# A planner's clock for DMA transposes, and one gate item moved in an encoder trunk

## The chip, the cores and the metric

The kernel runs on one core of a Trainium2 chip. The metric is the device time of one execution in microseconds (us); lower is better. Times are given as the median of several runs. Beside them one execution was taken by the hardware profiler, and all rows below come from that one.

The engines of a core are named PE (TensorE, matmuls), PEld (its weight loads), DVE (VectorE), ACT (ScalarE), POOL (GpSimd) and SP (SyncE). In this kernel SP issues every DMA, in the order of its instruction stream; SPq marks such an issue.

## The reference, cut to what matters

A bidirectional encoder of two layers is applied with the same weights to two groups of requests, each of 512 rows of 1024 columns, all in float32:

```python
def encoder_layer(x, c, ...):
    shift, scale, gate = split(silu(c) @ w_ada + b_ada, 3)
    h = rmsnorm(x, g_norm) * (1 + scale) + shift
    qa, ka, va, ga, qb, kb, vb, gb = split(h @ w_in)      # 512 x4, 256 x2, 512 x2 columns
    # mixer A: 8 heads of 64, rotary; three dilated windows, merged by their softmax denominators
    ya = merged(dilated_attention(rope(qa)/8, rope(ka), va, w, d)
                for w, d in ((128,1), (512,4), (2048,16))) * silu(ga)
    # mixer B: 4 heads, key 64, value 128; decaying retention forward + backward, group RMS norm
    r = retention(rope(qb), rope(kb)/8, vb, decay_fwd) + reversed retention(decay_bwd)
    yr = r * rsqrt(mean(r*r)) * silu(gb)
    return x + gate * (concat(ya, yr) @ w_out)

def trunk(x, c, ...):                                     # for x_prompt and x_sample
    for l in range(2): x = encoder_layer(x, c, ...)
    return rmsnorm(x, g_final)
```

## The kernel before, in words

**Numbers and matmuls.** A float32 factor is split into a high and a low part that TensorE multiplies quickly; a product takes three matmuls (high x high, high x low, low x high). The split of a weight tile is one ACT copy (`wH`) and one DVE subtraction (`wL`). Activations stand transposed in `hT`, one pair of tiles for each k (eight of them) and batch b (two).

**Items.** The input projection of a layer is cut into 20 items, written out in `ORDER0` (layer 0) and `ORDER1` (layer 1): `p` a pair of attention heads' q and k, `v` the same pair's values, `r` and `w` the q, k and the values of two retention heads, `g` a gate. For each item and batch PE runs "main" matmuls from `hT` and the item's weights: a gate item has 24 for each batch (eight k's, three matmuls each). Items are taken in the order of the list; weights are loaded (`loader`) and split (`prepper`) in the same order. The last three items run batch by batch, all of batch 0 first. Then the out projection follows (`wo`, `yT`), 48 matmuls for each tile of 128 rows.

**Background.** What follows from an item is written as generators that are spawned when its main matmuls are issued: `rope` rotates q and k, stores them in DRAM (`stk_dram`) and loads them again as stacks (`QS`, `KS`, `KL`); `attn` multiplies scores; `soften` takes the exponential, writes the probabilities as two 16-bit tiles `pt` and issues a DMA transpose of each, `pT<-pt`; `attn_pv` multiplies the transposed probabilities with the transposed values (`vn<-vt`, also a DMA transpose) in a group of 24 matmuls; `value`, `rvalue`, `ret`, `r_out` and `gate` are the others. `mod_task` computes modulation vectors from `w_ada` tiles (`wa`) in eight steps for each of two tasks; they start at list positions `EX0` = 4 and `EX1` = 9 of layer 0. `outputs` spawns the loads and splits of `w_out` (`rawo`, `wo`) and the splits of y (`yT`) at list position 15 (`LN - LATE`).

**The planner.** Every engine's stream is fixed when the kernel is built. `Engine` passes each instruction on and tells `Plan.note` its estimated cost; `Plan.free` holds the time at which each engine's queue is free by that clock, `Plan.ready` when a tile is there. Before each step of main work `pump` issues background steps whose conditions hold by that clock. A condition is a time: `plan.at(tiles)` is the time at which the tiles are there and a slack by their maker, 1500 ns for a DMA (`SLACK`). The DMA part of the clock is one number, `Plan.dma`, the end of the last booked transfer: an ordinary issue books its bytes after it (an issue costs 450 ns, or 650 ns where neither side is in DRAM), and its landing is 770 ns later. So the clock sets the order of all queues, PE's above all, and what the chip does with that order is not fed back.

Buffers are heaps: `NHALF` = 48 tiles of 4 KB a partition, of which `W_T` may hold 10 (transposes and their sources), and 8 PSUM banks, 5 for main work and 3 for the background.

Of the kernel before, what the change touches and what calls it, by code (L numbers as in the profile page):

```python
# [27 lines left out]
NHALF = 48  # L28
NTURN = 10
NSURE = 3  # L30
ORDER0 = "g0 p0 g4 g5 v0 r0 w0 p1 v1 r1 w1 p2 v2 p3 v3 g1 g6 g7 g2 g3"
ORDER1 = "p0 v0 g0 r0 w0 p1 v1 g1 r1 w1 p2 v2 p3 v3 g4 g5 g6 g7 g2 g3"
EX0 = 4
EX1 = 9
# [113 lines left out]
class Plan:  # L148
# [37 lines left out]
        t = self.soon(*tiles)  # L186
        return 0.0 if t <= self.free[eng] else t

    def note(self, eng, cost, outs, ins, nbytes=0.0):
        part = eng == "SP" and (outs[0].shape[0] < P or outs[0].tensor.name.startswith("stk"))  # L190
        outs = [k for a in outs for k in self.keys(a)]
        ins = [k for a in ins for k in self.keys(a)]
        start = self.free[eng]
        for k in ins:
            start = max(start, self.seen(eng, self.ready.get(k)))
        for k in outs:
            if not (part and self.last.get(k, (0.0, ""))[1] == "DMA"):
                start = max(start, self.seen(eng, self.last.get(k)))
        if self.dead.intersection(outs + ins):
            raise RuntimeError("use of a spare buffer")  # L200
        end = start + cost
        self.free[eng] = end
        if eng == "SP":
            self.dma = max(end + 650.0, self.dma) + nbytes
            end = self.dma + 770.0
            eng = "DMA"
        for k in outs:
            self.ready[k] = (max(end, self.ready.get(k, (0.0, ""))[0]), eng)
        for k in outs + ins:
            if end >= self.last.get(k, (0.0, ""))[0]:  # L210
                self.last[k] = (end, eng)
# [190 lines left out]
class Engine:  # L402
# [5 lines left out]
    def __getattr__(self, op):  # L408
        fn = getattr(self.eng, op)

        def call(*args, **kw):
            r = fn(*args, **kw)  # L412
            outs = [a for k, a in kw.items() if k in self.OUT and hasattr(a, "tensor")]
            ins = [a for k, a in kw.items() if k not in self.OUT and hasattr(a, "tensor")]
            pos = [a for a in args if hasattr(a, "tensor")]
            if "out" in kw:
                ins += pos
            else:
                outs = pos[:1] + outs
                ins = pos[1:] + ins  # L420
            nbytes = 0.0
            if self.name == "SP":
                nbytes = outs[0].free_size() * outs[0].shape[0] * (2.0 / 290.0 if outs[0].dtype == F16 else 4.0 / 345.0)
            self.plan.note(self.name, self.cost(op, outs, ins), outs, ins, nbytes)
            return r
        return call

    def cost(self, op, outs, ins):
        out = outs[0]
        n = out.free_size()  # L430
        psum = any(a.tensor.name.startswith("banks") for a in ins)
        if self.name == "PE":
            c = 0.4219 * n
            self.strip, last = -1, self.strip
            if op == "transpose":
                return max(108.0, 2 * c)
            if ins[0].dtype == F32:
                if out.shape[0] > 32:
                    return max(4 * c, 60.0)
                self.strip = out.offset // out.ap[0][0] // 32  # L440
                return 27.0 if self.strip > last >= 0 else 4 * c
            return 0.5 * c if out.shape[0] == 64 else c + 12.0
        if self.name == "DVE":
            wide = [a for a in ins if a.free_size() > 1]
            fast = len(wide) <= 1 and not psum and op != "tensor_reduce"
            if op == "tensor_reduce":
                n = wide[0].free_size()
            extra = 0.0
            if n > 64 and not psum and (op == "scalar_tensor_tensor" or fast):
                extra = 65.0 * sum(1 for a in ins if a.free_size() == 1) + (60.0 if fast else 0.0)  # L450
            return 66.0 + n * (0.53 if fast else 1.05) + extra
        if self.name == "ACT":
            extra = sum(1 for a in outs[1:]) + sum(1 for a in ins if a.free_size() == 1)
            return (53.0 if psum else 93.0) + 93.0 * extra + 0.833 * n
        if op == "dma_start_transpose":
            return 1250.0 * n / 1024
        return 450.0 if any("dram" in str(a.tensor.name) for a in ins + outs) else 650.0


# [1 line left out]
def trunk_kernel(  # L461
# [364 lines left out]
    KINDS = {"p": "PQK", "v": "PV", "r": "RQK", "w": "RV", "g": "G"}  # L826
    ITEMS = [[(KINDS[x[0]], int(x[1])) for x in order.split()] for order in (ORDER0, ORDER1)]
    EARLY = 4
# [656 lines left out]
```

## Time and profile before

| | |
|---|---|
| median of 3 runs | 1066.94 us (1066.64 to 1071.24) |
| the profiled execution's own time | 1068.72 us |
| its span | 1066.9 us |
| granted TensorE clock over the span | 0.999 of full speed |
| PE busy | 1043.9 us, 5476 matmuls |
| PEld busy | 829.9 us |
| DVE busy | 766.8 us |
| ACT busy | 465.3 us |
| q1, the queue of all these DMAs | 188.69 MB, 62.4% of 16 DMA engines' time |
| DMA transposes | 64 `pT<-pt`, 8 `vn<-vt` |

Busy is the time in which an engine has at least one instruction under way; matmuls overlap, so the sum of their durations is more. The span is the time from the first to the last instruction of the execution that was profiled; its own time has 1.8 us around the span. Stretches are given in us from the start of the span. Layer 0's input projection ends at about 474 us, its out projection at about 565 us; layer 1's input projection ends at about 971 us.

### The profile page before, as it was taken

Reading aid. Unit: us, or ns where it says so; the run is one execution under the profiler, and the core shown is the slowest. Engines: PE = TensorE matmul, PEld = TensorE weight load, DVE = VectorE, ACT = ScalarE, POOL = GpSimd, SP = SyncE. Lnnn points to the kernel's source line nnn. Section 1 sums busy time; section 2 is a strip of 40 time slices with the busy share of each in tenths; the row PEclk is TensorE's granted clock in tenths of the full one; section 3 lists DMA queues with packets and bytes.
Section 4 is the critical chain, followed back from the end, with each engine's and each line's share of the span. In section 5 each row is a group of like instructions: output and inputs, shape, how many; then the busy total and the mean of one; then the engine's idle time right before and its main releaser. Section 6 shows DMA issues by size and latency. Waiting matters only on the chain.

```text
span 1066.9 us, 14779 instructions
## 1 busy us (share of the span) xinstructions
PE 1043.9 (98%) x5476; PEld 829.9 (78%) x5476; DVE 766.8 (72%) x1578; ACT 465.3 (44%) x807; POOL 0.2 (0%) x4
## 2 busy tenths in 40 slices
PE   8999999999999998999999999999999999999997
PEld 4778687777767876778888878878888787778886
DVE  5587766699668896674457885589857897776555
ACT  6364424326432565571234552427433375753011
POOL 0000000000000000000000000000000000000000
PEclk9999999999999999999999999999999999999999
DMA  8747895259964699933221796047941669962222
GB/s 350 295 139 180 238 302 209 73 194 260 273 228 139 160 244 241 234 110 137 89 90 62 240 208 221 21 139 195 244 154 51 224 119 261 244 166 99 97 101 79
DMA packets 209143, 189.63 MB, mean 178 GB/s; under 512 B 156656, under 2 KB 156944, under 8 KB 209072
## 3 DMA queue, kind: packets, MB, share of 16 engines
q1 hardware_dynamic: 209072, 188.69, 62.4%
q8 instruction: 43, 0.70, 0.3%
q14 instruction: 28, 0.23, 0.1%
HBM read 117.34 MB, written 33.57 MB: 141 GB/s over the span
## 4 chain that ended last, share of the span: by engine, by line
PE 77%; DVE 10%; DMA 6%; ACT 2%; SPq 2%; issue 2%; ACTq 0%; DVEq 0%
PE banks L412 77%; SPq L412 2%; DMA wa<-in_w_ada_dram 2%; DVE sS L412 2%; DMA pT<-pt 2%; DVE sd L412 1%; DVE pt L412 1%; DMA KL<-stk_dram 1%; DVE wL L412 1%; DVE yr L412 1%; ACT pt L412 1%; DVE rc L412 1%; DVE rs L412 1%; DVE rsq L412 1%; ACT wH L412 1%
## 5 line engine op out<-in xcount | busy, mean ns | idle before, releaser
L412 PE MATMUL banks<-hT,wH 128*128 128x512 f32 x1536 | 478.7, 392 | 0.6 <-DVE hT L412 0.2
L412 PEld LDWEIGHTS banks<-hT,wH 128*128 128x128 f32 x1536 | 285.3, 188 | 74.4 <-issue 14.1
L412 PE MATMUL banks<-hT,wL 128*128 128x512 f32 x768 | 299.2, 390 | 1.3 <-DVE wL L412 1.3
L412 PE MATMUL banks<-wo,yT 128*128 128x512 f32 (+1 forms) x792 | 175.8, 383 | 0.0
L412 PEld LDWEIGHTS banks<-hT,wL 128*128 128x128 f32 x768 | 144.2, 188 | 32.0 <-DVE wL L412 1.8
L412 PEld LDWEIGHTS banks<-wo,yT 128*128 128x128 f32 x792 | 145.2, 188 | 28.9
L412 PE MATMUL banks<-wH,hT 128*128 128x256 f32 x512 | 97.5, 284 | 0.0
L412 PEld LDWEIGHTS banks<-wH,hT 128*128 128x128 f32 x512 | 81.8, 191 | 4.8 <-issue 3.8
L412 ACT ACTIVATE sS<-sS,sm 128x512 f32<-128x512 f32 x100 | 71.1, 712 | 32.9 <-DVE sm L412 31.9
L412 DVE SCALAR_TENSOR_TENSOR pt<-sS,sm,pt 128x512 f16<-128x512 f32 x100 | 69.9, 747 | 5.0 <-DMA stk_dram<-rs 2.6
L412 PE MATMUL banks<-wL,hT 128*128 128x256 f32 x256 | 72.4, 283 | 0.0
L412 DVE TENSOR_TENSOR wL<-raw,wH 128x1024 fp32r<-128x1024 f32 x56 | 68.1, 1219 | 5.2 <-ACT wH L412 5.1
L412 ACT ACTIVATE wH<-raw 128x1024 fp32r<-128x1024 f32 x56 | 58.5, 1053 | 24.8 <-DMA raw<-in_w_in_dram 23.3
L412 ACT ACTIVATE pt<-sS,sm 128x512 f16<-128x512 f32 x100 | 65.8, 709 | 8.0 <-DVE sm L412 7.0
L412 DVE CUSTOM_DVE_ANT_0 sS<-banks,tabs 128x512 f32<-128x512 f32 x100 | 64.6, 685 | 5.7 <-PE banks L412 5.5
L412 ACT ACTIVATE sq<-xr 128x1024 bf16<-128x1024 f32 (+2 forms) x18 | 17.3, 963 | 116.4 <-DVE xr L412 92.0
L412 DVE TENSOR_TENSOR res<-banks,gb 128x512 f32<-128x512 f32 (+1 forms) x33 | 22.1, 671 | 55.1 <-PE banks L412 55.1
L412 PE MATMUL banks<-pT,vn 128*64 128x512 f16 x384 | 46.0, 381 | 5.4 <-DMA pT<-pt 5.4
L412 PEld LDWEIGHTS banks<-wL,hT 128*128 128x128 f32 x256 | 49.0, 191 | 1.0
L412 PE MATMUL banks<-sr,rv 128*128 128x512 f32 x164 | 46.0, 394 | 0.0
L412 PEld LDWEIGHTS <-vn 128*64 128x64 f16 x384 | 21.3, 109 | 27.4 <-issue 11.8
L412 PE MATMUL banks<-QS 128*128 128x512 f32 x96 | 38.1, 396 | 0.1
(309 smaller groups left out, 1215.7 us busy)
## 6 DMA issues: line engine op xcount, KB each, us to landing
raw<-in_w_in_dram SPq DMA_DIRECT2D x56, 512.0 KB, 4.7
wa<-in_w_ada_dram SPq DMA_DIRECT2D x48, 512.0 KB, 6.8
QS<-stk_dram SPq DMA_DIRECT2D x48, 256.0 KB, 4.5
KS<-stk_dram SPq DMA_DIRECT2D x48, 256.0 KB, 5.1
KL<-stk_dram SPq DMA_DIRECT2D x45, 256.0 KB, 4.6
stk_dram<-rs SPq DMA_DIRECT2D x36, 256.0 KB, 2.9
rawo<-in_w_out_dram SPq DMA_DIRECT2D x16, 512.0 KB, 4.5
stk_dram<-rc SPq DMA_DIRECT2D x24, 256.0 KB, 5.0
```

Source lines behind the costliest of these rows:

```text
L412: r = fn(*args, **kw)
```

## The change: what it does

- `Plan.note` gets a flag for DMA transposes. For one, the queue of SP is taken as occupied until the later of its own cost and 770 ns after the end of all booked transfers; the transfers are then booked until 1400 ns after that, and the tile is there 2200 ns after it. Before, a transpose was booked as any transfer: its queue was free after its cost, and its bytes (0.5 MB, 1.81 us) were added to the booked transfers.
- The cost of a transpose goes from 1250 to 1175 ns for each 1024 columns; both kinds of tile have 2048.
- In layer 0's list the item `g1` stands between `v1` and `r1`, no more between `v3` and `g6`. `EX0`, `EX1` and `LATE` stay as they are. `ORDER1` is not touched.

```diff
-ORDER0 = "g0 p0 g4 g5 v0 r0 w0 p1 v1 r1 w1 p2 v2 p3 v3 g1 g6 g7 g2 g3"
+ORDER0 = "g0 p0 g4 g5 v0 r0 w0 p1 v1 g1 r1 w1 p2 v2 p3 v3 g6 g7 g2 g3"
...
-    def note(self, eng, cost, outs, ins, nbytes=0.0):
+    def note(self, eng, cost, outs, ins, nbytes=0.0, turned=False):
...
         end = start + cost
         self.free[eng] = end
-        if eng == "SP":
+        if eng == "SP" and turned:
+            self.free[eng] = end = max(end, self.dma + 770.0)
+            self.dma = end + 1400.0
+            end += 2200.0
+            eng = "DMA"
+        elif eng == "SP":
             self.dma = max(end + 650.0, self.dma) + nbytes
             end = self.dma + 770.0
             eng = "DMA"
...
-            self.plan.note(self.name, self.cost(op, outs, ins), outs, ins, nbytes)
+            self.plan.note(self.name, self.cost(op, outs, ins), outs, ins, nbytes, op == "dma_start_transpose")
...
         if op == "dma_start_transpose":
-            return 1250.0 * n / 1024
+            return 1175.0 * n / 1024
```

## Rows read from the trace of the kernel before

**Rows 1.** The page: engines' busy us, share of the span, instructions.
```profile
PE 1043.9 (98%) x5476; PEld 829.9 (78%) x5476; DVE 766.8 (72%) x1578; ACT 465.3 (44%) x807; POOL 0.2 (0%) x4
```

**Rows 2.** Busy us of each engine (and instructions) in the last stretch.
```profile
1060.00:1067.00 7.00, 0.00 (x0) 0.00 (x0) 2.74 (x14) 1.23 (x3) 0.00 (x0) 0.79 0.20 75
```

**Rows 3.** PE's waits: us, times, longest; whole span, last line 270 to 310.
```profile
PE banks L412 <- DMA pT<-pt: 5.4, 5, 2.3
...
PE banks L412 <- DMA KL<-stk_dram: 1.7, 3, 1.1
...
PE banks L412 <- DMA wa<-in_w_ada_dram: 1.9, 2, 1.6
```

**Rows 4.** Timeline of PE: start, us, instruction, count, idle before and releaser.
```profile
299.67 2.21 PE L412 MATMUL banks<-wa,siluT 128*32 128x512 f32 x8 [1.62 <-DMA wa<-in_w_ada_dram]
...
407.15 0.62 PE L412 MATMUL banks<-pT,vn 128*64 128x512 f16 x4 [0.69 <-DMA pT<-pt]
410.07 2.32 PE L412 MATMUL banks<-pT,vn 128*64 128x512 f16 x19 [2.31 <-DMA pT<-pt]
...
414.00 0.51 PE L412 MATMUL banks<-KL,QS 128*128 128x512 f32 x1 [1.07 <-DMA KL<-stk_dram]
...
436.39 2.35 PE L412 MATMUL banks<-pT,vn 128*64 128x512 f16 x20 [1.84 <-DMA pT<-pt]
```

**Rows 5.** Tiles pT, then raw: issue ns min/median/max; us to landing.
```profile
L412 SPq DMA_TRANSPOSE pT<-pt x64: 1597/2661/6569, 84.8 to 940.8; - x64
...
DMA to landing us min/median/max: 4.2/4.6/8.3
...
L412 SPq DMA_DIRECT2D raw<-in_w_in_dram x56: 328/424/1191, 5.5 to 915.8; - x56
...
DMA to landing us min/median/max: 3.4/4.7/10.6
```

**Rows 6.** Timeline of SP's DMA issues, two stretches: start, us occupied, count.
```profile
264.61 0.53 SPq L412 DMA_DIRECT2D stk_dram<-th  x1
...
273.72 1.68 SPq L412 DMA_DIRECT2D wa<-in_w_ada_dram  x2
275.49 13.13 SPq L412 DMA_TRANSPOSE pT<-pt  x4
...
386.85 0.92 SPq L412 DMA_DIRECT2D QS<-stk_dram  x2
...
390.30 0.60 SPq L412 DMA_DIRECT2D raw<-in_w_in_dram  x1
391.00 5.23 SPq L412 DMA_TRANSPOSE pT<-pt  x1
```

**Rows 7.** Timeline of PE: two steps (one k each) of a gate item.
```profile
414.35 0.62 PE L412 MATMUL banks<-hT,wH 128*128 128x512 f32 x2
...
415.03 0.62 PE L412 MATMUL banks<-hT,wH 128*128 128x512 f32 x2
```

**Rows 8.** Busy us in stretches: PE, PEld, DVE, ACT, POOL; clock, DMA share, GB/s.
```profile
227.00:257.00 30.00, 30.00 (x145) 22.37 (x144) 29.59 (x66) 16.69 (x34) 0.00 (x0) 1.00 0.93 220
...
257.00:342.00 85.00, 82.48 (x484) 61.59 (x483) 60.74 (x104) 34.28 (x57) 0.00 (x0) 1.00 0.75 223
342.00:400.00 58.00, 58.00 (x268) 46.78 (x267) 54.63 (x122) 32.92 (x68) 0.00 (x0) 1.00 0.79 208
400.00:474.00 74.00, 68.03 (x331) 52.27 (x330) 50.03 (x90) 42.74 (x73) 0.00 (x0) 1.00 0.86 203
```

**Rows 9.** Last PV group and first out projection of layer 0; splits of wo and y.
```profile
453.87 2.78 PE L412 MATMUL banks<-pT,vn 128*64 128x512 f16 x24
...
474.39 10.82 PE L412 MATMUL banks<-wo,yT 128*128 128x512 f32 x47
...
L412 DVE TENSOR_TENSOR wo<-rawo,wo x8: 1217/1219/1225, 439.6 to 472.3; 128x1024 fp32r<-128x1024 f32 x8
...
L412 DVE TENSOR_TENSOR yT<-yr,yT x9: 679/684/687, 474.0 to 483.2; 128x512 fp32r<-128x512 f32 x9
```

## The prediction

> **What bounds the kernel now.** I read the engine totals first: PE is busy 1043.9 of 1066.9 us [rows 1], so at most 23.0 us of the span are idle time of TensorE, and no edit of an order removes a matmul. The last 7 us, without any PE work [rows 2], are the last norm and the stores. What is idle at the start lies before the change can act on the clock, since the first transpose is issued at 84.8 us [rows 5]. What is left is read from the list of PE's waits: 5.4 us on `pT` (a transposed probability tile), 1.7 us on `KL`, and 1.9 us on `wa` around 270 to 310 us [rows 3], together 9.0 us. That is the whole prize. The timeline of PE shows where most of it lies, all in layer 0: 1.62 us at 299.67, 0.69 and 2.31 us in one group of 24 PV matmuls at 406 to 412, 1.07 us on `KL` just behind it, and 1.84 us in the next PV group at 436.39 [rows 4]. PE runs its stream in the order that the planner wrote. A PV group that stands too early in it therefore stops everything behind it, main matmuls that were ready included.
>
> Then the queue of SyncE. A transpose occupies its issuer for 1.6 to 6.6 us (median 2.66), an ordinary 512 KB load for 0.33 to 1.19 us (median 0.42), while both land at a median of 4.6 and 4.7 us [rows 5]. The long ones stand behind ordinary transfers: four transposes behind two `wa` loads hold the queue for 13.13 us, one behind a `raw` load for 5.23 us [rows 6]. The clock of the kernel before gives each 2.50 us (1250 ns per 1024 columns, 2048 columns), whatever is ahead. So the planner believes that the queue is free, and the tiles landed, earlier than they are.
>
> **The change part by part.**
>
> *The clock.* It removes and adds no instruction; it changes what the planner believes, and so the order of every queue after the first transpose. I work its hold out for two bursts, with the kernel's own constants (256 KB book 0.76 us of transfer, 512 KB 1.52 us, the first starts 0.65 us after its issue ends, a landing is 0.77 us later). Burst at 275.49: between 264.61 and 275.4 twelve 256 KB and three 512 KB transfers are issued, of which the first and the last stand in [rows 6], 12 x 0.76 + 3 x 1.52 = 13.7 us from about 265.7, so the last lands at 280.15 by the clock. The first transpose is held 280.15 - 275.49 = 4.66 us, the other three 2.35 us each: 11.7 us, against 10.0 by the old clock and 13.13 in the trace. The new clock finds 1.7 of the missing 3.1 us. The landing of the last moves less: old 288.7 (a transpose booked 1.81 us of transfer and the 0.77 us), new 287.2 + 2.2 = 289.4, a gain of 0.7 us. Burst at 391.00: six 256 KB loads and one of 512 KB from 386.85 [rows 6] run by the clock to 394.0, so the hold is 3.8 us against 2.5 old and 5.23 measured: 1.3 of 2.7 us found, and the landing moves only from 396.7 to 397.0. So about half of the hold becomes visible for what is queued behind a transpose, and a third or less for the tile itself. A PV group also has 1.5 us of slack in its condition (`SLACK`), which covers the rest in the first burst and not where such errors add up, as from 391 to 412.
>
> What each wait is worth by that:
> - `wa` at 270 to 310, 1.9 us: it is queued behind the 13.13 us burst and needs the queue, not the tile; 1.7 us are now foreseen. I take 1.8 gained, bounds 0 and 1.9.
> - `pT` around 291, the part of the 5.4 us that the named groups of [rows 4] leave (5.4 - 4.84 = 0.56): 0.4 gained, bounds 0 and 0.6.
> - `pT` at 406 to 436, 4.84 us: a quarter, 1.2, because landings move by 0.3 to 0.7 us a burst; bounds 0 and 4.8.
> - `KL`, 1.7 us, queue again: half, 0.9; bounds 0 and 1.7.
>
> The sum is 1.8 + 0.4 + 1.2 + 0.9 = 4.3 us. When a wait goes, a main matmul stands in its place and nothing is late next at once, since 0.68 us of ready main work stand for every three matmuls [rows 7]. A re-dealt order can also put a tile earlier than it lands elsewhere, because an unhindered transpose now lands after 2.35 + 2.2 = 4.55 us instead of 2.50 + 0.65 + 1.81 + 0.77 = 5.73. Measured are 4.2 at the least and 4.6 in the median [rows 5], which the slack covers; I take 0, between a gain of 0 and a loss of the same size as the waits that stay, 4.7 us.
>
> *The gate.* g1 is 48 matmuls of 128x512, sixteen steps of 0.68 us: 10.9 us of PE [rows 7]. They move from behind v3 to between v1 and r1, with one 512 KB weight load on SyncE's queue, the split of that weight on ACT and DVE, and two gate tasks, all of which are done at the old place today and cost the same at the new one; the queue loses the load behind v3, where it is held by transposes, and has it ahead of r1. The list positions move with it: the second modulation task still starts behind v1, and the loads of `w_out` are spawned one item earlier in the list, before v3, which in time is the same place because everything from r1 on stands 10.9 us later. Where it goes, DVE has no room (29.59 of 30.0 us) and has been the limit for the background work, so main matmuls are welcome there. Behind that DVE idles: 60.74 of 85 us, then 54.63 of 58, then 50.03 of 74 [rows 8]. Where it leaves, PE has 10.9 us less main work to cover the attention of pair 3. Its cost there is bounded by 0 (the cover lasts) and 10.9 us (the attention stays as far behind v3 as it was). I take 0: the last PV group starts at 453.87, the out projection at 474.39 [rows 9], so a shift of 10.9 us still ends before it, and DVE has 24.0 idle us in that stretch.
>
> Sum: -4.3 us, nothing for the gate. The profiled execution took 1068.72 us with a span of 1066.9; the median of the runs is 1066.94, so I take the sum off that: **1062.6 us**.
>
> **The rivals.**
>
> *All of the idle goes.* The gate puts 10.9 us of main work where DVE was full, bursts fall behind other loads, and PV groups come after their tiles everywhere: 1066.9 - 9.0 = 1057.9 us; I put it at 1058.5. For it: it is ten waits of 2.3 us at most [rows 3]. Against it: the clock still sees only half of a hold.
>
> *The waits stay.* What is late is not what the clock now sees: 1066.9 us. For it: the landing estimates move by 0.3 and 0.7 us only, and groups of [rows 4] were late by more. Against it: each of these waits stands behind a held queue. The Trainium skill, "Advanced Engine Details and Errata", section on the X-bar transpose, says that transposes are as fast as regular DMAs on this chip; by that the hold would be no property of the transpose and the sum would be 0. The trace agrees on the time to landing, 4.6 against 4.7 us, and not on the time at the issuer, 2.66 against 0.42 us [rows 5].
>
> *Slower: the out projection waits for its inputs.* The eight splits of `w_out` on DVE need the heap space that the attention holds, and the last starts at 472.3; nine splits of y tiles follow from 474.0, while PE begins the out projection at 474.39 [rows 9]: its inputs come just in time already. If the attention of pair 3 keeps its distance to v3, all of them come 10.9 us later, and an earlier PE only waits longer. The end then moves by the shift less what DVE's idle time takes back: with half of it taken back the out projection starts 5.5 us later than before, 1066.9 + 5.5 = 1072.4, with nothing taken back 1077.8. The kernel gets slower than before from the point where the first y tiles are split later than 474 us. Against it: the 24.0 idle us of DVE ahead of that point.
>
> **How the numbers follow.** Chances: forecast 40%, all idle goes 27%, waits stay 15%, slower 18%. Less than 0.5% (5.3 us, 1061.6 to 1072.3) is what a measurement of this kernel can't tell from no change. The forecast's own range is 1060.5 to 1065.5, and a fifth of it lies under 1061.6: faster 27 + 8 = 35%, within 32 + 15 = 47%, slower 18%. The range reaches from 1057.5, where nearly the whole 9.0 us are gone, to 1071, which leaves out most of the slower case and a little of the fastest.
>
> **What would show it.** Right: the list of PE's waits no longer has `wa` in layer 0 and has some 3 us of `pT` left; the out projection of layer 0 starts some 4 us before 474.4; layer 1, whose list is the same, hardly changes. The clock is wrong if transposes behind loads no longer hold the queue, or if `pT` waits stay at 5 us or grow. The gate is wrong if PE idles between the last gate matmul and the first `wo` matmul of layer 0, on `yT` or `wo`. The whole is wrong if new waits of several us appear in layer 1, where I price the re-dealing at 0.

## The result and the profile after

The kernel after takes 1058.81 us (median of 6 runs, 1057.38 to 1061.97), the kernel before, run beside it, 1067.62 us (6 runs, 1066.64 to 1072.65). The ratio is 0.9912, 95% interval [0.9887, 0.9938]: 0.9% faster. The profiled execution took 1060.97 us with a span of 1059.1, so the medians differ by 8.8 us and the spans by 7.8.

The page of the kernel after, its span and engine totals, against [rows 1]:

```profile
span 1059.1 us, 14785 instructions
...
PE 1044.4 (99%) x5476; PEld 829.1 (78%) x5476; DVE 765.5 (72%) x1578; ACT 462.5 (44%) x803; POOL 0.2 (0%) x4
```

PE does the same 5476 matmuls in the same busy time (1044.4 against 1043.9 us). What shrank is its idle time. PE's waits in the kernel after from 75 us on (us in total, times, longest), against [rows 3]:

```profile
PE banks L417 <- DMA KS<-stk_dram: 0.6, 1, 0.6
PE banks L417 <- DMA pT<-pt: 0.4, 1, 0.4
PE banks L417 <- DMA KL<-stk_dram: 0.4, 1, 0.4
PE banks L417 <- DMA wa<-in_w_ada_dram: 0.2, 1, 0.2
```

That is 1.6 us against 9.0: 7.4 of the 7.8 us by which the span is shorter. Ten waits became four, and the longest is 0.6 us. PE's timeline shows where the time came from. First the start of layer 1's main matmuls in the kernel before, then what answers to it and to [rows 4, 9] in the kernel after (start, us, instruction, count, idle time before and its releaser):

```profile
565.07 0.62 PE L412 MATMUL banks<-hT,wH 128*128 128x512 f32 x2
```

```profile
284.69 1.05 PE L417 MATMUL banks<-wa,siluT 128*32 128x512 f32 x4 [0.17 <-DMA wa<-in_w_ada_dram]
...
398.02 2.78 PE L417 MATMUL banks<-pT,vn 128*64 128x512 f16 x24
...
425.55 2.78 PE L417 MATMUL banks<-pT,vn 128*64 128x512 f16 x24
...
463.24 4.24 PE L417 MATMUL banks<-wo,yT 128*128 128x512 f32 x18
467.41 2.78 PE L417 MATMUL banks<-pT,vn 128*64 128x512 f16 x24
470.12 6.19 PE L417 MATMUL banks<-wo,yT 128*128 128x512 f32 x26
...
556.85 0.62 PE L417 MATMUL banks<-hT,wH 128*128 128x512 f32 x2
```

Layer 1 begins at 556.85 instead of 565.07: 8.2 us earlier, so the whole gain is made by the end of layer 0, and layer 1 gives 0.4 back. (About 0.7 us of it stands ahead of 75 us, where no transpose has been issued yet: PE waits 4.7 us there against 5.4, so that part is not the change's.) A PV group of 24 matmuls now runs in one piece of 2.78 us; the groups of [rows 4] were broken by waits. The last PV group of layer 0 stands inside the out projection, behind 18 of its matmuls, and nothing waits there.

The queue of SyncE did not get shorter. The transposes of tile `pT` (issuer's ns min/median/max, against [rows 5]) and two single ones on SP in the kernel after:

```profile
L417 SPq DMA_TRANSPOSE pT<-pt x64: 1565/2617/6341, 84.6 to 934.3; - x64
```

```profile
265.32 4.45 SPq L417 DMA_TRANSPOSE pT<-pt  x1
...
273.36 5.23 SPq L417 DMA_TRANSPOSE pT<-pt  x1
```

A transpose holds its issuer as long as before (median 2617 against 2661 ns), and single ones behind loads still take 4.45 and 5.23 us. The chip does the same; what changed is how far PE's stream stays behind it (numbers under the step that failed).

DVE, on the other hand, still has no room where the gate went. Busy us in stretches of the kernel after (PE, PEld, DVE, ACT, POOL with instructions; granted clock, DMA share, GB/s), against [rows 8]:

```profile
227.00:257.00 30.00, 30.00 (x141) 22.22 (x140) 29.53 (x69) 19.12 (x41) 0.00 (x0) 1.00 0.95 251
257.00:342.00 85.00, 84.78 (x497) 65.07 (x496) 57.69 (x95) 30.09 (x49) 0.00 (x0) 1.00 0.72 212
```

### The profile page after: what moved, and what is told of

Same layout as the page of the kernel before. It is cut to its first block, busy times and chain, and to the rows that moved or that the text cites. A ratio compares the mean times of both kernels' runs of the same rounds, so it can differ in the third digit from the quotient of the medians.

```text
span 1059.1 us, 14785 instructions
## 1 busy us (share of the span) xinstructions
PE 1044.4 (99%) x5476; PEld 829.1 (78%) x5476; DVE 765.5 (72%) x1578; ACT 462.5 (44%) x803; POOL 0.2 (0%) x4
## 4 chain that ended last, share of the span: by engine, by line
PE 83%; DVE 7%; DMA 5%; SPq 2%; ACT 1%; issue 1%; ACTq 0%; DVEq 0%
PE banks L417 83%; SPq L417 2%; DMA KL<-stk_dram 1%; DMA stk_dram<-rc 1%; DVE pt L417 1%; DVE hT L417 1%; DVE sd L417 1%; DMA wa<-in_w_ada_dram 1%; DVE sS L417 1%; DVE rc L417 1%; DVE wL L417 1%; ACT wH L417 1%; DMA raw<-in_w_in_dram 1%; DMA stk_dram<-yr 0%; DMA x<-in_x_prompt_dram 0%
## 5 line engine op out<-in xcount | busy, mean ns | idle before, releaser
L417 PE MATMUL banks<-wo,yT 128*128 128x512 f32 (+1 forms) x744 | 165.7, 383 | 0.0
L417 PEld LDWEIGHTS banks<-wo,yT 128*128 128x128 f32 x744 | 136.2, 188 | 27.4 <-ACT wH L417 0.4
L417 ACT ACTIVATE sS<-sS,sm 128x512 f32<-128x512 f32 x90 | 63.9, 712 | 25.0 <-DVE sm L417 24.6
L417 DVE CUSTOM_DVE_ANT_0 sS<-banks,tabs 128x512 f32<-128x512 f32 x90 | 58.9, 685 | 12.3 <-PE banks L417 6.2
L417 DVE SCALAR_TENSOR_TENSOR pt<-sS,sm,pt 128x512 f16<-128x512 f32 x90 | 63.6, 745 | 0.4 <-ACT pt L417 0.4
L417 ACT ACTIVATE pt<-sS,sm 128x512 f16<-128x512 f32 x90 | 59.6, 709 | 2.8 <-DVE sm L417 1.8
L417 ACT ACTIVATE sq<-xr 128x1024 bf16<-128x1024 f32 (+2 forms) x15 | 14.2, 944 | 94.4 <-DVE xr L417 65.1
L417 PEld LDWEIGHTS banks<-sr,rv 128*128 128x128 f32 x166 | 30.5, 188 | 8.5 <-issue 2.5
```

## The experiments

Theory H (the hold): a transpose keeps SyncE's queue until the transfers ahead have landed; the new clock sees it, so what is queued behind comes in time, and that is the gain. Rival N (no hold): only the tile's landing counts, and any order that places PV groups later does as well. Rival G (the gate): the gate's place is what pays. Rival D (the deal): any small change of the clock deals a new order, and the result is one draw. Waits below are PE's from 75 us on, as for the kernel after; their sum stood at 9.0 us before. Ratios are to the kernel before, with their 95% intervals.

### The hold by itself

**e4_hold_alone** leaves out the whole computation: groups of 0 to 4 loads of 512 KB, then three transposes of the kernel's size, then one load behind them, all on SP's queue, twice over.

```python
for i in range(n):
    nc.sync.dma_start(raw[i], w_in[0, (step + i) % 28])
for a, b in zip(src, dst):
    nc.sync.dma_start_transpose(out=b..., in_=a...)
nc.sync.dma_start(fol, w_in[1, step % 28])
```

> A program that leaves out the whole computation: three transposes of one 128x2048 16-bit tile each, directly behind 0, 1, 2, 3 or 4 loads of 512 KB on the same queue, then one load, each group after the one before has landed. If a transpose holds its issuer until the transfers ahead have landed: the first of three takes about 2 us with nothing ahead and then 1.5 us more for each load ahead, some 4, 5.5, 7 and 8.5 us; the second and third take 1.6 to 2.7 us in every group; the load behind starts only after all three. If the hold is the transpose's own cost and chance: the first takes the same 1.6 to 3 us whatever is ahead.

SP's timeline, the first transpose behind 0, 1, 2, 3 and 4 loads (start, us at the issuer):

```profile
4.12 1.42 SPq L488 DMA_TRANSPOSE pT<-pt  x1
...
16.00 3.39 SPq L488 DMA_TRANSPOSE pT<-pt  x1
...
29.37 4.28 SPq L488 DMA_TRANSPOSE pT<-pt  x1
...
44.53 5.71 SPq L488 DMA_TRANSPOSE pT<-pt  x1
...
62.97 5.91 SPq L488 DMA_TRANSPOSE pT<-pt  x1
...
73.85 0.60 SPq L489 DMA_DIRECT2D behind<-in_w_in_dram  x1
```

The second pass gives 1.80, 3.51, 4.34, 6.49 and 6.91 us. Each issue ends with the landing of the last load ahead: 16.00 + 3.39 = 19.4, and that load, issued at 15.55, landed 4.0 us later, at 19.6; for four loads 62.97 + 5.91 = 68.9 against 61.22 + 7.8 = 69.0. The other two transposes of a group take 1.8 to 3.6 us each (7.13 us for three with nothing ahead); all but one of them end within 0.5 us of the landing of the transpose ahead, as at 21.47 against 21.52. The load behind starts only after all three, at 73.85. So the hold exists, and it is one of the queue, not of the tile: the transposes read nothing that the loads wrote. H stands on this point. The size expected per load ahead, 1.5 us, was 2.0 and 1.7 us for the first load and on average 0.8 and 1.1 for each further one (first and second pass).

### The two parts alone

**e1_clock_only**, the kernel after with the old list:

```diff
-ORDER0 = "... v1 g1 r1 w1 p2 v2 p3 v3 g6 g7 g2 g3"
+ORDER0 = "... v1 r1 w1 p2 v2 p3 v3 g1 g6 g7 g2 g3"
```

> The new clock with the gate item at its old place. If the clock alone brings the gain (what PE waits for is tiles behind a held queue, and an order that knows the hold has no such waits), about 1059 us and under 2 us of PE waits on DMAs after 80 us. If the two parts need each other, most of the DMA waits go but a new wait of 3 to 4 us stands near the start of the second retention (about 257 us, where the main matmuls have run out of the background's results and g1 would have filled in), and the time is 1061 to 1064 us. If the order was only dealt anew and came out lucky, anything, with DMA waits of several us at other places.

Measured: 0.9951 [0.9934, 0.9968], 1061.7 us. PE's waits, its timeline (the place of the waits, then a PV group), and SP's queue ahead of them:

```profile
PE banks L417 <- DMA wa<-in_w_ada_dram: 2.3, 2, 1.6
PE banks L417 <- DVE wL L417: 1.3, 1, 1.3
PE banks L417 <- DMA pT<-pt: 0.2, 1, 0.2
```

```profile
274.59 1.05 PE L417 MATMUL banks<-wa,siluT 128*32 128x512 f32 x4 [1.64 <-DMA wa<-in_w_ada_dram]
...
276.28 1.05 PE L417 MATMUL banks<-wa,siluT 128*32 128x512 f32 x4 [0.64 <-DMA wa<-in_w_ada_dram]
...
418.07 2.78 PE L417 MATMUL banks<-pT,vn 128*64 128x512 f16 x24
```

```profile
264.74 5.52 SPq L417 DMA_TRANSPOSE pT<-pt  x1
...
270.31 1.05 SPq L417 DMA_DIRECT2D wa<-in_w_ada_dram  x2
```

The profiled execution, 1065.12 us, is the slowest of its five. The clock alone removes the `pT` waits (5.4 to 0.2 us) and those on `KL`. What is left, 3.6 of 3.8 us, is one place between 264 and 276 us, at the second retention's values: their split `wL` comes late, and then `wa`, which was issued behind a transpose that held the queue for 5.52 us. This is the second of the expected cases, in place, size and time. The PV group of 406 us [rows 4], the sixth of layer 0, now stands at 418.07.

**e2_gate_only**, the kernel before with the new list:

> The gate item at its new place with the old clock. If the gate alone brings the gain: about 1059 us. If the clock is what counts: DMA waits of PE of 5 us or more stay, 1065 to 1069 us. The slower rival of the prediction (the out projection waits for its inputs, since 10.9 us less main work cover the last pair's attention) would show here: a wait on wo or yT of 5 to 9 us at the start of layer 0's out projection, and 1070 us or more.

Measured: 1.0039 [1.0024, 1.0054], 1071.35 us, slower than before. Waits 9.1 us, of which 5.9 on `pT`. PE's timeline at the end of layer 0's list, SP's just ahead of it, and the stretch behind in busy us:

```profile
473.68 0.40 PE L412 MATMUL banks<-pT,vn 128*64 128x512 f16 x1
...
477.64 1.06 PE L412 MATMUL banks<-pT,vn 128*64 128x512 f16 x4 [3.55 <-DMA pT<-pt]
...
480.16 4.16 PE L412 MATMUL banks<-pT,vn 128*64 128x512 f16 x19 [1.46 <-DMA pT<-pt]
```

```profile
464.27 6.01 SPq L412 DMA_DIRECT2D raw<-in_w_in_dram  x4
...
472.58 5.06 SPq L412 DMA_TRANSPOSE pT<-pt  x2
```

```profile
477.00:484.00 7.00, 4.91 (x23) 2.29 (x22) 2.02 (x3) 2.22 (x5) 0.00 (x0) 0.51 0.40 74
```

The last PV group of pair 3 stands inside the out projection and stops it for 5.0 us: its transposes were issued at 472.58, behind four loads. Then 19 of its matmuls take 4.16 us, against 2.32 in [rows 4], at a granted clock of 0.51. So the gate by itself, with the old clock at 1250, does harm, and G as the whole cause falls.

### Later places alone

**e3_slack_3us**, the kernel before with every DMA's slack at 3.0 us, so that each consumer is placed later and no hold is known:

```diff
-SLACK = {..., "DMA": 1500.0}
+SLACK = {..., "DMA": 3000.0}
```

> The kernel before with 3.0 us of slack on every DMA-made tile in place of 1.5. If what matters is only that a PV group is placed later, the waits on pT go as well as with the new clock and the time comes within 2 us of it, 1058 to 1061 us. If the clock must know the hold, because the loads behind a transpose (wa, KL, KS) and the sum of several holds are late by more than 3 us, waits of 3 us or more stay and the time is 1063 to 1067 us.

Measured: 1.0016 [1.0002, 1.003], 1068.51 us. The waits fall from 9.0 to 5.0 us, and the time does not. PE's timeline, SP's queue ahead of it, and busy us in the stretch (the column behind POOL's is the granted clock):

```profile
297.38 0.62 PE L412 MATMUL banks<-pT,vn 128*64 128x512 f16 x4 [1.98 <-DMA pT<-pt]
...
300.43 4.42 PE L412 MATMUL banks<-pT,vn 128*64 128x512 f16 x19 [2.42 <-DMA pT<-pt]
```

```profile
287.03 10.83 SPq L412 DMA_TRANSPOSE pT<-pt  x3
```

```profile
298.60:305.40 6.80, 4.97 (x21) 2.45 (x21) 2.14 (x3) 1.66 (x3) 0.00 (x0) 0.50 0.74 249
```

Three transposes hold the queue for 10.83 us, which 1.5 us more of slack does not cover: 4.4 of the 5.0 us are this one group. The granted clock also falls to 0.50 for 6.8 us, from within the second wait on, and 19 matmuls take 4.42 us against 2.32 in [rows 4]; that takes back 2.1 us of what the shorter waits give. At this slack, placing later was no substitute for knowing the queue, so this form of N falls as far as one order can show it; another slack was not run.

### The hold line taken out

**e5_no_hold_1200** and **e6_hold_1200** are a pair: both are the kernel after at 1200 ns for each 1024 columns, and only the first lacks the hold.

```diff
-            self.free[eng] = end = max(end, self.dma + 770.0)      # e5 alone
+            pass
...
-            return 1175.0 * n / 1024                               # e5 and e6
+            return 1200.0 * n / 1024
```

> The changed kernel with the one line of the hold taken out (a transpose frees the queue after its own cost; its booking of 1400 and landing of 2200 ns stay) and its cost at 1200 instead of 1175 ns per 1024 columns. The planner itself foresees no wait of PE over half a us in this order, so what PE waits for shows errors of the clock alone. Hold theory: the waits on DMA tiles (pT, wa, KL, KS) come back, 4 us or more in all after 80 us, 1063 to 1067 us. Re-deal theory (the order of after is simply lucky, any order without a foreseen wait does as well): under 2.5 us of such waits, 1058 to 1061 us.

> The changed kernel with the cost alone at 1200: the pair of the run without the hold, and a neighbour that shows how much of the gain hangs on the very order. Hold theory: under 2.5 us of waits on DMA tiles after 80 us, 1058 to 1061 us. If the changed kernel's order was luck: several us of waits, 1062 us or more.

Measured: e5 1.0143 [1.0118, 1.0168], 1083.35 us; e6 0.994 [0.9919, 0.996], 1060.97 us. All of PE's waits, first of e5, then of e6:

```profile
PE banks L417 <- DMA pT<-pt: 17.3, 4, 8.1
PE banks L417 <- DMA wa<-in_w_ada_dram: 0.9, 1, 0.9
```

```profile
PE banks L417 <- DVE sr L417: 0.7, 1, 0.7
```

**e12_no_hold_1150** and **e11_hold_1150** are the same pair at 1150 ns.

> The changed kernel without the line of the hold, at 1150 ns. Without it the clock books a lone transpose to land 2.30 + 2.20 us after its issue, earlier than the old clock did, and nothing adds for what lies ahead. If that is what cost 17 us of waits on pT at 1200: 10 us or more of them again, 1070 us or more. If it was the deal: under 5 us and 1060 to 1066 us.

> The changed kernel with the cost alone at 1150: one more neighbour with the hold in its clock. If the hold makes the outcome dependable: under 2.5 us of waits on DMA tiles, 1058 to 1061 us, as at 1175 and 1200. If the new clock is a matter of chance too: 4 us or more, 1063 us or more.

Measured: e12 1.0136 [1.0109, 1.0162], 1083.11 us, with 16.5 us of waits (`pT` 10.2); e11 0.9936 [0.9915, 0.9957], 1061.92 us, with 3.0 (2.7 on DMA tiles), both just outside what was expected of a dependable clock.

One line makes 1083.35 - 1060.97 = 22.4 us in one pair and 1083.11 - 1061.92 = 21.2 in the other. e5 came out far slower than the 1063 to 1067 us expected of it: PE waits 17.5 us more than in e6, and it is busy 4.7 us longer (1049.3 against 1044.6 us) for the same matmuls, with two stretches of 6.8 us at a granted clock of 0.50 (290.6 to 297.4 and 915.3 to 922.1 us). The difference has to be read with what the other new lines do: without the hold they book a transpose's landing 2.2 us after its own cost, earlier than the clock before did, and e5 and e12 came out slower than the kernel before. What is shown is that this booking works with the hold and not without it.

### The old booking with other constants

**e7_old_clock_1175_gate** (the kernel before with the new list and 1175, no hold), **e9_old_clock_1150_gate** (the same at 1150) and **e10_old_clock_1175** (1175 with the old list):

```diff
-            return 1250.0 * n / 1024
+            return 1175.0 * n / 1024          # e7, e10; 1150.0 in e9
...
-ORDER0 = "... v1 r1 w1 p2 v2 p3 v3 g1 g6 g7 g2 g3"      # e7 and e9
+ORDER0 = "... v1 g1 r1 w1 p2 v2 p3 v3 g6 g7 g2 g3"
```

> The kernel before with the gate item at its new place and a transpose at 1175 ns, still booked as any transfer, without the hold. Here too the planner foresees no wait over half a us, the out projection included, so it is the gate's move without the wait at the out projection that the move alone at 1250 ns ran into. Hold theory: 4 to 9 us of waits on DMA tiles, 1063 to 1067 us. If the place of the gate is what brings the gain: 1058 to 1061 us.

> A neighbour of the order that came out fastest (old clock, gate item at its new place, a transpose at 1175): the same at 1150 ns per 1024 columns. If the old clock with the gate moved is as good a planner as the new one: again under 2 us of waits on DMA tiles after 75 us and 1056 to 1060 us. If that order was a lucky deal, as the wait of 9 us at 1250 suggests: 4 us or more of waits, 1062 us or more.

> The kernel before with the cost of a transpose alone at 1175 ns, nothing else. If the smaller cost by itself is what helps: 1058 to 1062 us. If the old clock leaves what waits there are to chance: 3 to 10 us of waits on DMA tiles, 1063 to 1069 us.

Measured: e7 0.9901 [0.9879, 0.9923], 1056.7 us; e9 0.992 [0.9896, 0.9944], 1058.82 us; e10 1.001 [0.9996, 1.0024], 1069.92 us. PE's waits of e7, then of e9, then of e10:

```profile
PE banks L412 <- DMA KL<-stk_dram: 0.6, 2, 0.3
```

```profile
PE banks L412 <- DMA KS<-stk_dram: 1.0, 1, 1.0
PE banks L412 <- DMA pT<-pt: 0.5, 1, 0.5
```

```profile
PE banks L412 <- DMA pT<-pt: 3.6, 3, 2.6
PE banks L412 <- DMA wa<-in_w_ada_dram: 3.5, 1, 3.5
```

e7 is a miss for H as I had put it: without a hold, the gate and 75 ns off one constant take nearly all waits away. It beats the kernel before, and from the kernel after it can't be told apart (0.9901 [0.9879, 0.9923] beside 0.9912 [0.9887, 0.9938], each against its own runs of before). e10 says that the constant alone does nothing; e9 says that e7 is not the only such order, e2 that the gate alone is not enough. So under the old booking the three deals with the gate in its new place have 9.1, 0.6 and 1.5 us of waits: D holds there. Of the 5.4 us between the spans of the kernel after and e7 (1059.1 and 1053.7) the waits explain 1.0. The rest lies in PE's busy time, 1039.6 against 1044.4 us for the same 5476 matmuls; why they took less in that order stays open.

### The gate at another place

**e8_gate_before_p2**, the kernel after with `g1` behind the second retention's values instead of ahead of its q and k:

```diff
-ORDER0 = "... v1 g1 r1 w1 p2 v2 p3 v3 g6 g7 g2 g3"
+ORDER0 = "... v1 r1 w1 g1 p2 v2 p3 v3 g6 g7 g2 g3"
```

> The changed kernel with the gate item between w1 and p2, behind the second retention's items, instead of ahead of r1. If the gate is needed near 257 us because main work runs out there: a wait of some 2 to 4 us between 240 and 300 us and 1061 to 1063 us. If any place ahead of pair 3 does: 1058 to 1061 us and under 2.5 us of waits.

Measured: 0.9959 [0.9945, 0.9973], 1063.31 us, with 0.9 us of waits (`KL` 0.5, `wa` 0.2, `KS` 0.2) and a span of 1059.1 us, that of the kernel after. The wait of e1 at the retention's values is gone although the gate is behind them, so it was not the gate's cover that removed it there. The profiled execution took 1060.88 us, below this kernel's median, and its rows don't explain why the others were longer: the waits came out as in the second expected case, the time did not.

## Why the prediction was right and wrong

**The bound** held for this change: of the 9.0 us of waits 7.4 went, and PE's busy time stayed. As a bound on every order it was wrong: e7 is 11.6 us below the kernel before (1056.7 against 1068.31), because PE's busy time fell too. And the case that came was the rival "all of the idle goes", put at 1058.5 us with a chance of 27%, and not the forecast of 1062.6, whose own range of 1060.5 to 1065.5 misses 1058.81. The outer range of 1057.5 to 1071 holds it only because it was drawn to take in that rival.

**The step that failed** is the term "`pT` at 406 to 436, 4.84 us: a quarter, 1.2, because landings move by 0.3 to 0.7 us a burst". All of it went (`pT` 5.4 to 0.4 us, and the 0.4 lies in layer 1), and with the clock alone too (0.2 us in e1). I had kept the old order and moved estimates in it by a few tenths, each burst from the time at which the chip issued it. A changed clock deals a new order instead: the sixth PV group stands at 406.05 us before, at 418.07 in e1 and at 425.55 in the kernel after (where 10.9 us of gate matmuls have moved ahead of it). Its last transpose on SP, in the kernel before, in e1 and in the kernel after:

```profile
405.74 1.60 SPq L412 DMA_TRANSPOSE pT<-pt  x1
```

```profile
410.19 4.97 SPq L417 DMA_TRANSPOSE pT<-pt  x1
```

```profile
419.04 3.31 SPq L417 DMA_TRANSPOSE pT<-pt  x1
```

So the group stood 0.3 us behind the issue of a tile that it needs, and now stands 7.9 and 6.5 us behind it. By the prediction's own sums the old clock asks for 5.73 + 1.5 = 7.2 us there and the new one for 4.55 + 1.5 = 6.05: the planner's clock was about 7 us off at this group (an estimate), and with the hold it is about right. The prediction said that the errors add up from 391 to 412 us and then priced the shift of a single burst. Counted in the traces over all sixteen PV groups, from the start of the last of a group's four transposes to the group's first matmul (negative where the matmul starts first), the smallest distance is 2.9 to 4.6 us in the five orders of the new clock (3.3 in the kernel after), -2.1 to 4.2 in the six of the old booking (0.3 before, 4.2 in e7), and -2.4 and -0.6 in e5 and e12. Every group that waits 1.8 us or more for `pT` has a distance of at most 3.4 us.

**`wa`**, 1.8 us predicted: 1.9 to 0.2, so 1.7. The number is right and the reason is not shown: with the clock alone PE waits 2.3 us on `wa`, at 274.59 and 276.28, behind a held queue as before. In the kernel after, the gate or the other deal took it away; no run tells them apart.

**`KL`**, 0.9 us: 1.7 to 0.4, with 0.6 us on `KS` in its place, 0.7 net.

**Re-dealing in layer 1**, taken at 0: right. Its waits go from 0.7 to 1.0 us, and it gives back 0.4 us of layer 0's 8.2.

**The gate at nothing**: wrong, and a fixed price was the wrong form. With the new clock it gives 1061.7 - 1058.81 = 2.9 us (ratios 0.9951 and 0.9912, whose intervals touch at 0.9934 and 0.9938); with the old clock at 1250 it costs 0.4%; with the old booking at 1175, e10 against e7, it gives about 1.1%. The parts don't add.

**The slower rival** did not come in the change, where nothing waits around 463 to 476 us. It came in e2, at the place named, the out projection, but on `pT` and not on `yT` or `wo`: the last PV group was placed inside the out projection before its transposes had landed. That its price was nearly met (1071.35 against 1072.4 us) is luck: the waits of e2 add up to those of the kernel before (9.1 and 9.0 us), and PE is busy 2.7 us longer.

**"The waits stay"** fell with the result (9.0 to 1.6 us), and the reading by which the hold is no property of the transpose fell with e4. The Trainium skill, "Advanced Engine Details and Errata", section on the X-bar transpose, says that transposes are as fast as regular DMAs on this chip. The runs agree for the landing alone (medians 4.6 and 4.7 us [rows 5]); the issuer is held from 1.4 us with nothing ahead to 5.9 behind four loads.

**What is shown and what is open.** Shown: the hold is real; the new booking is worth some 21 to 22 us more with it than without it; and over the orders that were run, the new clock is more even, in time and in the distances above. Its five (the kernel after, e1, e6, e8, e11) lie between 0.9912 and 0.9959; the six of the old booking (the kernel before, e2, e3, e7, e9, e10) between 0.9901 and 1.0039, two of them as fast; eleven orders are few, and the gate's place and the constant differ among them. Open: whether e7 and e9 are good because of the gate's place or by the luck of the deal, and so how much of this change's gain needed the hold at all.

## What to carry to other kernels

A planner that fixes the order of in-order queues must know what holds a queue, not only when a tile lands: measure both for each kind of transfer by itself, as e4 does, before tuning the order. Price a change of such a clock by all the waits that it can reach and not by shifting the old order, since the order is dealt anew. Read from the trace how far each consumer stands behind the issue of its last input, and compare it with what the clock asks for. And try the neighbours of a constant before crediting a mechanism, because one order is one draw.

## What the hardware showed that I had not expected

The hold ends within 0.3 us of the landing of the last load ahead, and back-to-back transposes hold each other: 7.13 us for three with no load ahead, 10.83 behind four loads.

A wait can cost more than its length. In e10 the granted clock fell to half, 1.2 of 2.4 GHz, about 1 us before the end of the 3.5 us wait on `wa`, and stayed there for 6.8 us; in the kernel before, behind the wait of 2.31 us [rows 4], the clock stayed at full. Busy us in stretches, first of e10, then of the kernel before (the column behind POOL's is the granted clock):

```profile
274.50:281.30 6.80, 5.78 (x19) 2.59 (x21) 3.68 (x8) 0.91 (x1) 0.00 (x0) 0.50 1.06 292
```

```profile
408.00:415.00 7.00, 3.79 (x24) 2.27 (x24) 2.73 (x11) 2.57 (x5) 0.00 (x0) 1.00 0.92 257
```

In e2 the half clock cost 4.16 - 2.32 = 1.8 us over 19 PV matmuls, in e3, behind waits of 1.98 and 2.42 us, 4.42 - 2.32 = 2.1 us.

The start varies too, far ahead of the first transpose. In the profile of e6 the clock was at 0.79 between 27 and 35 us, in that of the kernel after at 1.00, although both have the same list, PE had just waited 1.3 us for the same split `wL` in both, and the planner's changes act only from 84 us on:

```profile
27.00:35.00 8.00, 7.74 (x87) 5.64 (x88) 2.23 (x4) 0.15 (x1) 0.00 (x0) 0.79 1.03 408
```

```profile
27.00:35.00 8.00, 7.96 (x106) 5.55 (x110) 2.85 (x7) 1.39 (x2) 0.00 (x0) 1.00 1.03 406
```

In the same 8 us the records have 87 matmuls in one and 106 in the other. So two executions of orders this close can differ by such a stretch, and a verdict between them needs several runs of each.
